# A fixed TensorE order for the first memory attention of a two-layer streaming trunk

## The chip, the cores and the metric

The kernel runs on one core of one Trainium2 chip. The metric is the device time of one execution in microseconds (us). Before the change the median of three executions is 769.24 us (768.9 to 769.38).

## The reference

Two layers over 512 tokens of width 1024. The first layer mixes tokens with a chunkwise matrix memory (mLSTM, four heads of 256), the second with block-causal attention over a compressed key/value side. Each layer also attends to a fixed memory of 256 rows with four heads of 128; the first of these two memory attentions is what the change touches:

```python
def memory_attention(mq, mz, mk, mv, q_gain):
    bsz, s, _ = mq.shape
    q = rmsnorm(mq.reshape(bsz, s, MEM_HEADS, MEM_HEAD_DIM), q_gain)
    sc = jnp.einsum("bqhd,bkhd->bhqk", q, mk, preferred_element_type=jnp.float32) * (MEM_HEAD_DIM ** -0.5)
    p = jax.nn.softmax(sc, axis=-1).astype(mv.dtype)
    out = jnp.einsum("bhqk,bkhd->bqhd", p, mv).reshape(bsz, s, MEM_WIDTH)
    return out * jax.nn.silu(mz)
```

Beside it the layer projects its normed input to q and k (convolved, with SiLU), to v, and to two gates o and z, head by head, and needs the input and forget gates of the recurrence.

## The kernel before

Precision comes from splitting: every operand of a projection is held as a high part and a low part (`split`, lines 128 to 137: ScalarE copies the high part at L130, VectorE subtracts it at L131), and a product is three matmuls, two with the high weights (L157) and one with the low ones (L162). Weights come in pieces of 512 KB (`load`), each split in the same way into two buffers that take turns (wr, wh, wl).

The work of the layer is written as Python generators that yield at places where other work may stand in between, and `weave(main, side, plan)` runs a main generator and lets a side one advance `plan[i]` steps after the main one's step `i`, one step where the plan is over. In the stretch of the change the main chain is `a_qk(0)` (four projections of 24 matmuls each, two pieces of 12 with a yield after each and one more at the end; then a convolution of four taps on VectorE, L627 and L629, and a SiLU, L200 and L201), `a_v(0)` (the value projection, four weight pieces over four token tiles) and `a_oz(0)` (the gates of head 0). The side generator is `memory_and_gates`: six steps of `mem_attn`, and in the fourth the end of the recurrence's gates (L604 to L610).

Step `i` of `mem_attn` does three things for three heads: the transposes of head `i-1`'s probabilities (`trans`, eight at L368, then two splits), the scores of head `i` (`scores`, two att tiles of 12 matmuls in all, a row maximum at L328, a bias at L330, an exponential with row sum at L338 on ScalarE, a reciprocal at L339 and a scaling at L341), and the values of head `i-2` (`values`, six matmuls and a gating at L346). The att tiles are in two PSUM buffers, the transposes' tp tiles in two others.

The generators only set the order in which the program is written down. Before the change, a scheduler then places each engine's instructions by a timeline of its own, TensorE's among them, so that matmuls of the side generator stand in the middle of projections. On the chip each engine has one queue in the order that the scheduler gave it.

Of the kernel before, what the change touches and what calls it, by code (L numbers as in the profile page):

```python
# [40 lines left out]
def weave(main, side, plan=()):  # L41
    for i, _ in enumerate(main):
        for _ in range(plan[i] if i < len(plan) else 1):
            next(side, None)
    for _ in side:
        pass


def chain(*gens):
    for g in gens:  # L50
        yield from g


def drain(g):
    for _ in g:
        pass
# [3 lines left out]
def trunk(ctx: ExitStack, tc: tile.TileContext, pv_d, pos_d, x_d, mem_d, memT_d, wmem_d, wg_d, wa_d, woa_d,  # L60
# [20 lines left out]
    def st(shape, tag, bufs=1, dt=F32):  # L81
        return POOLS.get(tag, sp).tile(shape, dt, tag=tag, bufs=bufs, name=nm(tag))

    def wide(tag, bufs, dt=F32):

        t = st([P, 1056], tag, bufs, dt)
        return t[:, :NT * 258].rearrange("p (t c) -> p t c", t=NT)
# [4 lines left out]
    def s2(shape=(P, 512)):  # L92
        return st(list(shape), "s2", NS2)

    def acc(shape=(P, 512)):
        return pp.tile(list(shape), F32, tag="acc", bufs=4, name=nm("acc"))
# [26 lines left out]
    def col(name, i=0):  # L123
        o = _PV[name] + i
        return pv[:, o:o + 1]


    def split(hi, lo, src, scale=None):
        if scale is None:
            A.activation(hi, src, AF.Copy)  # L130
            V.tensor_tensor(out=lo, in0=src, in1=hi.bitcast(F32), op=ALU.subtract)  # L131
        else:
            A.activation(hi, src, AF.Identity, scale=scale)  # L133
            V.scalar_tensor_tensor(out=lo, in0=src, scalar=scale, in1=hi.bitcast(F32),  # L134
                                   op0=ALU.mult, op1=ALU.subtract)

    def load(src, nk, ncol, pieces=1, raw=None):
        n = nk * ncol
        if raw is None:
            raw = wp.tile([P, 1024], F32, tag="wr", bufs=2, name=nm("wr"))  # L140
            nc.sync.dma_start(raw[:, :n], src)
        hi = wp.tile([P, 1024], F32R, tag="wh", bufs=2, name=nm("wh"))
        lo = wp.tile([P, 1024], F32R, tag="wl", bufs=2, name=nm("wl"))
        for i in range(pieces):
            ps_ = slice(i * n // pieces, (i + 1) * n // pieces)
            split(hi[:, ps_], lo[:, ps_], raw[:, ps_])
        return (hi[:, :n].rearrange("p (k c) -> p k c", k=nk), lo[:, :n].rearrange("p (k c) -> p k c", k=nk))
# [41 lines left out]
    def proj_T(w, hT, ps):  # L189
        for k in range(0, KT, 4):  # L190
            prod([(ps, sub(hT, slice(None), j), sub(w, slice(None), j), False) for j in range(k, k + 4)],
                 k == 0, k == 4)
            yield
# [4 lines left out]
    def silu2(out, src, t=None):  # L198
        t = s2() if t is None else t
        A.activation(t, src, AF.Tanh, scale=0.5)  # L200
        V.scalar_tensor_tensor(out=out, in0=t, scalar=1.0, in1=src, op0=ALU.add, op1=ALU.mult)  # L201
# [147 lines left out]
    def mem_attn(mu, mkT, mv, yT):  # L349
        mq, sz, rq = mu  # L350
        prs, pTs = {}, {}

        def scores(h):
            prs[h] = []
            for j in range(2):
                ps = att([P, 2, 256])
                for t in range(2):
                    tt = 2 * j + t
                    prod([(ps[:, t], sub(mq[h // 2], slice(None), h % 2, slice(tt * P, (tt + 1) * P)),
                           sub(mkT, slice(None), h), True)], True, True)  # L360
                prs[h] += softmax_rows([ps[:, 0], ps[:, 1]], rq[:, 2 * j:2 * j + 2, h])

        def trans(h):
            pT = st([P, 2, S], "s4", 2, F32R), st([P, 2, S], ("gt", "z4")[h % 2], 1, F32R)
            for kt in range(2):
                tp = tps()
                for t in range(NT):
                    PE.transpose(tp[:, t * P:(t + 1) * P], prs[h][t][:, kt * P:(kt + 1) * P], ident)  # L368
                split(pT[0][:, kt], pT[1][:, kt], tp)
            pTs[h] = pT  # L370

        def values(h):
            ps = att()
            prod([(ps, sub(pTs[h], slice(None), kt), sub(mv, slice(None), kt, slice(h * P, (h + 1) * P)), False)
                  for kt in range(2)], True, True)
            gate_out(yT, 8 + h, ps, sz[h // 2][:, h % 2])

        for i in range(6):
            if 0 <= i - 1 < 4:
                trans(i - 1)  # L380
            if i < 4:
                scores(i)
            if 0 <= i - 2 < 4:
                values(i - 2)
            yield
# [228 lines left out]
    def a_qk(h):  # L614
        i0 = 4 + 20 * (h // 2) + 12 * (h % 2)
        r = 4 + 2 * (h % 2)
        for n, name in enumerate("qk"):
            heads[h][name] = st([P, 2, S], "qk", 4, F32R), yT[n][:, r:r + 2]
        for i in range(4):
            w = load(wa_d[i0 + i], KT, P)  # L620
            ps = acc()
            yield from proj_T(w, hT, ps)
            j = (8 if i >= 2 else 0) + 2 * h + i % 2
            tmp = st([P, 2, S], "kl")
            raw, u = tmp[:, 0], tmp[:, 1]
            A.activation(raw, ps, AF.Copy)
            V.tensor_scalar(u, raw, col("cw", 48 + j), col("cb", j), op0=ALU.mult, op1=ALU.add)  # L627
            for d in range(1, 4):
                V.scalar_tensor_tensor(out=u[:, d:], in0=raw[:, :S - d], scalar=col("cw", (3 - d) * 16 + j),  # L629
                                       in1=u[:, d:], op0=ALU.mult, op1=ALU.add)  # L630
            silu2(u, u, raw)
            hi, lo = heads[h]["qk"[i // 2]]
            split(hi[:, i % 2], lo[:, i % 2], u)
            yield

    def tok_proj(i0, evac):
        pss = [acc() for _ in range(NT)]
        for c in range(4):
            w = load(wa_d[i0 + c], 2, 512)
            yield from prod_tok(pss, lambda k, t: rows(hT, k, t), w, 2, 2 * c, c == 0, c == 3, evac)  # L640

    def a_v(pr):
        vs = []
        for j in range(2):
            v = wide("v", 2, F32R), st([P, NT, 256], "u4", 5, F32R)
            G.memset(v[0][:, :, 256:258].bitcast(F32), 1.0)
            heads[2 * pr + j]["v"] = v
            vs.append(v)

        def evac(t, ps):  # L650
            for j in range(2):
                split(vs[j][0][:, t, 0:256], vs[j][1][:, t], ps[:, j * 256:(j + 1) * 256])

        yield from tok_proj(8 + 20 * pr, evac)

    def a_oz(h):
        gt = st([P, NT, 256], ("gt", "z4")[h % 2])
        heads[h]["g"] = gt

        def evac(t, ps):  # L660
            th = s2()
            A.activation(th, ps, AF.Tanh, scale=0.5)
            V.scalar_tensor_tensor(out=th[:, 256:], in0=th[:, 256:], scalar=1.0, in1=ps[:, 256:],
                                   op0=ALU.add, op1=ALU.mult)
            V.scalar_tensor_tensor(out=gt[:, t], in0=th[:, :256], scalar=1.0, in1=th[:, 256:],
                                   op0=ALU.add, op1=ALU.mult)

        yield from tok_proj(4 + 20 * (h // 2) + (8, 16)[h % 2], evac)
# [82 lines left out]
    def memory_and_gates():  # L751
        for i, _ in enumerate(mem_attn(mu, mkT, mv, yT)):
            if i == 3:
                drain(gc)
            yield

    weave(chain(a_qk(0), a_v(0), a_oz(0)), memory_and_gates(), (1, 0, 0) * 6)
    weave(chain(a_qk(1), a_oz(1)), a_attn(0))
    rope_tables()
    weave(chain(a_qk(2), a_v(1), a_oz(2)), a_attn(1))  # L760
# [414 lines left out]
```

## Time and profile before

| | us |
|---|---|
| median of three executions | 769.24 |
| the profiled execution | 769.35 |
| its span, first to last instruction | 767.6 |
| what lies around the span | 1.75 |
| TensorE busy with matmuls | 755.0 (98% of the span) |
| VectorE busy | 484.1 (63%) |
| ScalarE busy | 409.4 (53%) |

PE is TensorE's matmuls, DVE is VectorE, ACT is ScalarE, POOL is GpSimd. In rows of the timeline the first number is the start in us from the span's start, the second the duration in us, then engine, line, operation, tiles written and read, shape, and how many alike follow each other; in square brackets stands how long the engine was idle before, and what ended that. A matmul's duration reaches over the start of the next, so that the work per matmul is read from start to start.

### The profile page before, as it was taken

The page shows a single profiled execution, that of the slowest core. Times are in us where ns is not written, and L with a number is a line of the kernel's source. Part 1 is how long each engine was busy: PE and PEld are TensorE (multiplying, and loading weights), DVE is VectorE, ACT ScalarE, POOL GpSimd, SP SyncE. Part 2 cuts the span into 40 slices and gives each one's busy share as a digit, 9 for nine tenths or more (in the row PEclk, how much of TensorE's full clock was granted, in tenths as well). Part 3 has the DMA queues.
Part 4 walks back from the last instruction along what each step waited for, and adds up shares of the span by engine and source line. Part 5 has one row for each costly group of instructions (what it writes and reads, how often), then busy time and mean ns, then how long its engine had stood idle before and what let it go on. Part 6 is the DMA issues. An engine that isn't in the chain of part 4 may idle for free.

```text
span 767.6 us, 10826 instructions
## 1 busy us (share of the span) xinstructions
PE 755.0 (98%) x3948; PEld 647.8 (84%) x3948; DVE 484.1 (63%) x945; ACT 409.4 (53%) x958; POOL 106.8 (14%) x159
## 2 busy tenths in 40 slices
PE   8999998999999999999999999999999999999998
PEld 6798887888888888888888887899888888888886
DVE  5743599547868836766434664566758697776422
ACT  6964557345446435536333658457856666644220
POOL 0131010010110101001001131020334230500000
PEclk9999999999999999999999999999999999999999
DMA  9523120322132222224443532121221111511241
GB/s 323 207 84 109 56 84 29 109 83 90 63 99 80 83 89 104 71 94 154 154 160 137 174 129 73 53 83 59 83 87 59 56 50 40 190 56 56 66 155 55
DMA packets 25909, 76.39 MB, mean 100 GB/s; under 512 B 3072, under 2 KB 3968, under 8 KB 25856
## 3 DMA queue, kind: packets, MB, share of 16 engines
q1 hardware_dynamic: 24144, 73.44, 28.4%
q10 hardware_dynamic: 1584, 2.25, 0.8%
q8 instruction: 31, 0.51, 0.3%
q14 instruction: 22, 0.18, 0.1%
q0 software_dynamic: 128, 0.01, 0.0%
HBM read 71.49 MB, written 4.19 MB: 99 GB/s over the span
## 4 chain that ended last, share of the span: by engine, by line
PE 85%; DVE 8%; ACT 3%; issue 1%; DMA 1%; POOL 0%; SPq 0%; ACTq 0%; DVEq 0%
PE acc L157 47%; PE acc L162 23%; PE att L157 3%; PE att L1031 2%; PE att L162 2%; DMA yTh<-in_wmem_dram 1%; DVE wl L131 1%; PE tp L1018 1%; DVE tiny L328 1%; ACT junk L187 1%; DVE kl L629 1%; ACT s L338 1%; PE tp L952 1%; PE att L715 1%; PE att L716 1%
## 5 line engine op out<-in xcount | busy, mean ns | idle before, releaser
L131 DVE TENSOR_TENSOR wl<-wr,wh 128x1024 fp32r<-128x1024 f32 (+5 forms) x117 | 136.2, 1165 | 152.9 <-ACT wh L130 126.7
L130 ACT ACTIVATE wh<-wr 128x1024 fp32r<-128x1024 f32 (+5 forms) x117 | 117.5, 1008 | 134.1 <-PE acc L157 123.8
L157 PE MATMUL acc<-wh,hTl 128*128 128x512 f32 (+3 forms) x320 | 113.3, 365 | 0.0
L157 PE MATMUL acc<-wh,hTh 128*128 128x512 f32 (+3 forms) x320 | 112.4, 367 | 0.3 <-ACT hTh L133 0.3
L157 PE MATMUL acc<-hTh,wh 128*128 128x512 f32 x256 | 101.8, 398 | 0.0
L157 PE MATMUL acc<-hTl,wh 128*128 128x512 f32 x256 | 100.3, 392 | 0.0
L157 PE MATMUL acc<-wh,yTh 128*128 128x512 f32 (+1 forms) x224 | 84.7, 382 | 0.0
L157 PE MATMUL acc<-wh,yTl 128*128 128x512 f32 (+1 forms) x224 | 84.5, 379 | 0.0
L162 PE MATMUL acc<-wl,hTh 128*128 128x512 f32 (+3 forms) x320 | 82.0, 364 | 0.0
L162 PE MATMUL acc<-hTh,wl 128*128 128x512 f32 x256 | 69.8, 392 | 0.0
L157 PEld LDWEIGHTS acc<-wh,hTh 128*128 128x128 f32 x320 | 59.1, 188 | 9.4 <-ACT hTh L133 0.6
L157 PEld LDWEIGHTS acc<-wh,hTl 128*128 128x128 f32 x320 | 59.6, 188 | 8.7 <-DVE hTl L134 0.2
L162 PEld LDWEIGHTS acc<-wl,hTh 128*128 128x128 f32 x320 | 56.5, 188 | 8.6
L162 PE MATMUL acc<-wl,yTh 128*128 128x512 f32 (+1 forms) x224 | 60.1, 378 | 0.0
L162 PEld LDWEIGHTS acc<-hTh,wl 128*128 128x128 f32 x256 | 47.6, 188 | 9.9 <-DVE wl L131 0.2
L157 PEld LDWEIGHTS acc<-hTh,wh 128*128 128x128 f32 x256 | 48.1, 188 | 9.1
L157 PEld LDWEIGHTS acc<-hTl,wh 128*128 128x128 f32 x256 | 48.2, 188 | 9.1
L157 PEld LDWEIGHTS acc<-wh,yTh 128*128 128x128 f32 x224 | 42.1, 188 | 7.2
L157 PEld LDWEIGHTS acc<-wh,yTl 128*128 128x128 f32 x224 | 42.1, 188 | 7.1
L162 PEld LDWEIGHTS acc<-wl,yTh 128*128 128x128 f32 x224 | 41.2, 188 | 7.4
L182 POOL TENSOR_SCALAR tiny<-tiny 128x8 f32<-128x8 f32 (+3 forms) x21 | 5.5, 262 | 245.1 <-ACT junk L187 68.2
L157 PE MATMUL acc<-wh,u 128*128 128x384 f32 (+1 forms) x160 | 37.8, 362 | 0.8 <-ACT u L133 0.7
(285 smaller groups left out, 1387.0 us busy)
## 6 DMA issues: line engine op xcount, KB each, us to landing
wr<-in_wa_dram SPq DMA_DIRECT2D x46, 512.0 KB, 3.2
wr<-in_wb_dram SPq DMA_DIRECT2D x16, 512.0 KB, 3.5
wr<-in_woa_dram SPq DMA_DIRECT2D x12, 512.0 KB, 3.2
wr<-in_wob_dram SPq DMA_DIRECT2D x12, 512.0 KB, 3.2
wr<-in_wmem_dram SPq DMA_DIRECT2D x8, 512.0 KB, 3.4
yTh<-in_wmem_dram SPq DMA_DIRECT2D x5, 512.0 KB, 7.3
yTl<-in_x_dram SPq DMA_DIRECT2D x4, 512.0 KB, 9.1
u<-in_x_dram SPq DMA_DIRECT2D x4, 512.0 KB, 6.2
```

What stands on the lines that cost most here:

```text
L130: A.activation(hi, src, AF.Copy)
L131: V.tensor_tensor(out=lo, in0=src, in1=hi.bitcast(F32), op=ALU.subtract)
L157: PE.matmul(ps, x if lhs else w_[0], w_[0] if lhs else x, start=start and id(ps) not in seen, stop=False)
L162: PE.matmul(ps, a_[0] if lhs else w_[1], w_[1] if lhs else a_[0], start=False, stop=stop and left[id(ps)] == 0)
L187: A.activation(j[:, :src.shape[-1]], src, AF.Square, scale=scale, accum_out=accum)
L328: V.tensor_reduce(mx[:, j:j + 1], ps, axis=AX.X, op=ALU.max)
L338: A.activation(out[j], ps, AF.Exp, bias=nb[:, j:j + 1], scale=rq[:, j:j + 1], accum_out=sm[:, j:j + 1])
L629: V.scalar_tensor_tensor(out=u[:, d:], in0=raw[:, :S - d], scalar=col("cw", (3 - d) * 16 + j), in1=u[:, d:], op0=ALU.mult, op1=ALU.add)
L715: PE.matmul(ps[:, :258], low(c, i), v[0][:, c], start=False, stop=False)
L716: PE.matmul(ps[:, :256], ph[:, blk(c, i)], v[1][:, c], start=False, stop=c == i)
L952: PE.transpose(tp[:, t * P:(t + 1) * P], main[:, t, h * P:(h + 1) * P], ident)
L1031: PE.matmul(ps[:, i * P:(i + 1) * P], vt[:, c, h * P:(h + 1) * P], pTs[h][:, o:o + P], start=c == 0, stop=c == i)
```

## The change

The weave of the stretch is put under a manual schedule for TensorE: its instructions stay in the order in which the generators write them, and the scheduler places only the other engines around them. The plan changes too: the six steps of the memory attention come after the main chain's steps 1, 5, 9, 13, 16 and 19 (before: 1, 4, 7, 10, 13 and 16), and none after that. Steps 1 to 12 are those of `a_qk(0)`, so that step four of the memory attention now comes after the first yield of the value projection, and steps five and six later in it.

```diff
-    weave(chain(a_qk(0), a_v(0), a_oz(0)), memory_and_gates(), (1, 0, 0) * 6)
+    with tc.manual_schedule(engines={mybir.EngineType.PE}):
+        weave(chain(a_qk(0), a_v(0), a_oz(0)), memory_and_gates(), (1, 0, 0, 0) * 3 + (1, 0, 0) * 2 + (1,) + (0,) * 20)
```

The number of instructions on each engine is the same. The orders of GpSimd and of the DMA queue on SyncE are the same row for row, those of VectorE and ScalarE are the same up to head 0's softmax (VectorE's up to L600 behind the scaling of its first half), and from the gate projection of head 0 on all orders are the same again. Three places show what moved.

TensorE behind the second of the four projections (its last four matmuls are the row acc_1060 before and acc_1062 now). Before, the third projection, acc_1155, came next, and head 0's transposes, L368, only in the fourth, acc_1261:

```order
L162 MATMUL acc_1060<-hTh_171,wl_1057 128x512 x4
L157 MATMUL acc_1155<-hTh_171,wh_1151 128x512
...
L157 MATMUL att_1089<-mkT_167,u_86_471 128x256
...
L162 MATMUL acc_1155<-hTh_171,wl_1152 128x512 x4
L157 MATMUL acc_1261<-hTh_171,wh_1257 128x512
L157 MATMUL acc_1261<-hTl_172,wh_1257 128x512
L368 MATMUL tp_1075<-ident,s_178_1006 128x128
L368 MATMUL tp_1082<-ident,s_178_1006 128x128
```

The same place now, with the transposes of both halves (s_178 and s_183) and head 1's scores (att_1103, att_1122) ahead of the third projection, acc_1157:

```order
L162 MATMUL acc_1062<-hTh_171,wl_1059 128x512 x4
L368 MATMUL tp_1089<-ident,s_178_1008 128x128 x2
L368 MATMUL tp_1089<-ident,s_183_1027 128x128 x2
L368 MATMUL tp_1096<-ident,s_178_1008 128x128 x2
L368 MATMUL tp_1096<-ident,s_183_1027 128x128 x2
L157 MATMUL att_1103<-mkT_167,u_86_471 128x256
...
L157 MATMUL att_1122<-mkT_167,u_86_471 128x256
...
L157 MATMUL acc_1157<-hTh_171,wh_1153 128x512
```

Head 0's transposes moved ahead by 38 matmuls of projections, to a place where nothing else stands between them and the second projection.

TensorE behind the third projection, now: head 1's transposes (s_197, s_202), head 2's scores (att_1208, att_1227) and head 0's values (att_1246) follow each other, and only then the fourth projection, acc_1263:

```order
L162 MATMUL acc_1157<-hTh_171,wl_1154 128x512 x4
L368 MATMUL tp_1194<-ident,s_197_1115 128x128 x2
L368 MATMUL tp_1194<-ident,s_202_1134 128x128 x2
L368 MATMUL tp_1201<-ident,s_197_1115 128x128 x2
L368 MATMUL tp_1201<-ident,s_202_1134 128x128 x2
L157 MATMUL att_1208<-mkT_167,u_88_473 128x256
...
L157 MATMUL att_1227<-mkT_167,u_88_473 128x256
...
L157 MATMUL att_1246<-s_190_1087,mv_169 128x512
...
L157 MATMUL acc_1263<-hTh_171,wh_1259 128x512
```

Before, head 0's values (att_1222) came after two weight pieces of the value projection for its first two token tiles; now they stand straight behind two tiles of scores. The two att buffers are held by those scores, so att_1246 takes the buffer of att_1208. The next step repeats the pattern with att_1342, att_1361 and att_1380.

VectorE now, from the scaling of head 1's second half to the bias of head 2's first scores:

```order
L341 TENSOR_SCALAR s_202_1134<-s_202_1134,tiny_1135 128x256 x2
L201 SCALAR_TENSOR_TENSOR kl_1141<-kl_1141 128x512
L131 TENSOR_TENSOR wl_1311<-wr_1308,wh_1310 128x1024
L131 TENSOR_TENSOR z_211_1193<-tp_1194,s_210_1192 128x512
L328 TENSOR_REDUCE tiny_1215<-att_1208 128x1 x2
L131 TENSOR_TENSOR yTh_173<-kl_1141,qk_975 128x512
L131 TENSOR_TENSOR z_211_1193<-tp_1201,s_210_1192 128x512
L330 SCALAR_TENSOR_TENSOR tiny_1218<-tiny_1215,rq_477 128x2
```

Seven instructions now stand between the scaling that lets head 1's transposes go and the bias that lets the exponentials of att_1208 go.

## Rows read from the trace of the kernel before

**Rows 1.** The page: busy time and share of each engine.
```profile
PE 755.0 (98%) x3948; PEld 647.8 (84%) x3948; DVE 484.1 (63%) x945; ACT 409.4 (53%) x958; POOL 106.8 (14%) x159
```

**Rows 2.** Whom TensorE waited for, 76 to 150 us: total, times, longest.
```profile
PE att L157 <- ACT s L338: 1.5, 2, 0.8
```

**Rows 3.** Busy time by windows: us, PE, PEld, DVE, ACT, POOL, PEclk, DMA share, GB/s.
```profile
96.00:110.00 14.00, 14.00 (x76) 11.95 (x75) 13.84 (x35) 8.12 (x19) 2.29 (x4) 1.00 0.34 112
```

**Rows 4.** Timeline of PE, 92 to 152 us: the third projection's first matmuls.
```profile
96.00 0.39 PE L157 MATMUL acc<-hTh,wh 128*128 128x512 f32 x1
96.23 0.39 PE L157 MATMUL acc<-hTl,wh 128*128 128x512 f32 x1
```

**Rows 5.** Timeline of DVE, 80 to 150 us: head 0's softmax.
```profile
103.00 0.60 DVE L341 TENSOR_SCALAR s<-s,tiny 128x256 f32<-128x256 f32 x2
103.52 0.41 DVE L600 TENSOR_SCALAR e<-e 4x512 f32<-4x512 f32 x1
103.86 0.74 DVE L328 TENSOR_REDUCE tiny<-att 128x1 f32<-128x256 f32 x2
104.52 0.14 DVE L339 RECIPROCAL tiny<-tiny 128x2 f32<-128x2 f32 x1
```

**Rows 6.** Timeline of PE: the three waits, and transposes and scores without one.
```profile
121.88 1.03 PE L368 MATMUL tp<-ident,s 128*128 128x128 f32 x8
122.67 0.36 PE L157 MATMUL att<-mkT,u 128*128 128x256 f32 x1
122.87 0.28 PE L157 MATMUL att<-mkT,qk 128*128 128x256 f32 x1
122.99 0.28 PE L162 MATMUL att<-v,u 128*128 128x256 f32 x1
...
124.31 0.50 PE L157 MATMUL att<-s,mv 128*128 128x512 f32 x1 [0.69 <-ACT s L338]
124.65 0.39 PE L157 MATMUL att<-z,mv 128*128 128x512 f32 x1
...
126.38 0.63 PE L604 MATMUL tp<-ident,e 128*128 128x128 f32 x4 [0.41 <-DVE gt L131]
...
128.18 0.50 PE L157 MATMUL att<-s,mv 128*128 128x512 f32 x1 [0.83 <-ACT s L338]
...
129.66 1.03 PE L368 MATMUL tp<-ident,s 128*128 128x128 f32 x8
```

**Rows 7.** Timeline of DVE: durations of the links, and head 3's first scaling.
```profile
109.38 0.74 DVE L629 SCALAR_TENSOR_TENSOR kl<-kl,pv 128x511 f32<-128x511 f32 x1
110.04 0.15 DVE L330 SCALAR_TENSOR_TENSOR tiny<-tiny,rq 128x2 f32<-128x2 f32 x1
110.11 1.28 DVE L131 TENSOR_TENSOR gt<-tp,s 128x512 fp32r<-128x512 f32 x2
...
113.35 1.21 DVE L131 TENSOR_TENSOR wl<-wr,wh 128x1024 fp32r<-128x1024 f32 x1
...
124.69 0.61 DVE L341 TENSOR_SCALAR s<-s,tiny 128x256 f32<-128x256 f32 x2
```

**Rows 8.** Timeline of ACT, 80 to 150 us: one tile's two exponentials, and two splits.
```profile
105.82 0.55 ACT L338 ACTIVATE s<-att,tiny,rq 128x256 f32<-128x256 f32 x1
...
106.81 0.20 ACT L338 ACTIVATION_READ_ACCUMULATOR s<-att,tiny,rq 128x1 f32 x1
...
108.11 1.08 ACT L130 ACTIVATE s<-tp 128x512 fp32r<-128x512 f32 x2
```

**Rows 9.** The last matmuls, and busy time and PEclk by windows at the end.
```profile
763.30 0.61 PE L162 MATMUL acc<-wl,yTh 128*128 128x512 f32 x2
...
766.00:766.50 0.50, 0.00 (x0) 0.00 (x0) 0.00 (x0) 0.00 (x0) 0.00 (x0) 1.00 0.42 156
...
767.00:767.60 0.60, 0.00 (x0) 0.00 (x0) 0.00 (x0) 0.00 (x0) 0.00 (x0) 0.50 0.00 0
```

**Rows 10.** Timeline of PE, 0 to 34 us: the first transposes.
```profile
1.81 4.34 PE L121 MATMUL tp<-ident 128*128 128x128 f32 x20 [1.81 <-POOL ident masks.py:199]
```

## The prediction

> **What bounds the kernel now.** I read the page's busy times first: TensorE works through 755.0 of 767.6 us [rows 1]. So the change, which moves matmuls and adds or removes none, can gain no more than TensorE's idle time, and all that it makes TensorE wait is lost, unless a later wait shrinks by it. Next the waits of the stretch in which the orders differ: two waits for ScalarE's exponentials, 1.5 us together [rows 2]; the timeline has them at 124.31 and 128.18 (0.69 and 0.83 us) with a third, 0.41 us, between them at 126.38 [rows 6]. That is the prize. Then the other engines there: from 96 to 110 us VectorE is busy for 13.84 of 14 us [rows 3], so a link of a softmax is done when its turn comes in VectorE's queue, not when its inputs are there. A fixed TensorE order is judged by that: where does TensorE now arrive before VectorE?
>
> **What goes.** The waits of 0.69, 0.41 and 0.83 us, 1.93 in all. After a wait the next matmul starts 0.34 us on (124.31 to 124.65) where 0.23 is the pace [rows 4, 6], so each costs 0.11 more: 2.3 us (an estimate). The moved matmuls cost the same elsewhere. DMAs and GpSimd keep their orders; weight pieces follow TensorE through their two buffers, so what TensorE loses they lose too, and nothing is fetched further ahead.
>
> **First new wait: head 0's transposes.** Behind the second projection TensorE stood at 96.00 before, and began the third [rows 4]. The work up to there is the same set of matmuls, so now it stands at 96.00 before the transposes. They read what L341 writes, and VectorE writes the first half at 103.00 to 103.60 [rows 5]. Nothing of VectorE's queue up to there moved, nor waits for what TensorE does after 96. Then comes L600 (to 103.86, where the next started), and as the two row maxima of 103.86 (0.66 us) now stand later, the reciprocal (0.14) and the second pair of L341 (0.60) end at about 104.65. Two of the eight transposes go at about 103.5, two by 104.75, the other four by 105.15, and with 0.1 at the change back to scores, head 1's scores start at 105.3. Without waiting they would start 0.79 + 0.09 after 96.00, at 96.9 (eight transposes take 121.88 to 122.67, and the first score's 0.20 is 0.08 over the 0.12 of the next) [rows 6]. Loss: **8.4 us**. Before, the third projection and half of the fourth filled this time; now they stand behind the transposes.
>
> That loss needs the projections to stay behind. The trace shows it: at 128.18 TensorE ended 0.83 us of waiting for one matmul, while the transposes behind it, whose first inputs VectorE had scaled by 125.3 [rows 7], started only at 129.66 [rows 6]. The Trainium skill, "TensorE: Matmul & The Clock Gate", section "Step-by-step: what each phase is for", says why one might hope otherwise: TensorE pulls weight loads ahead, but the matmuls "stay in program order". If more than loads could pass, the sum would be the 2.3 us gained; the rows side with the page's second half.
>
> **Second: head 1's transposes.** Scores (12 by 0.12) and the third projection (24 by 0.23) bring TensorE from 105.3 to 112.2. VectorE meanwhile needs, from 104.65: L201 (taken as a split beside it, 0.60), three splits of 0.60 to 0.65, three taps L629 (0.66 each), L627, two pairs of row maxima (0.66 each), and the scalings [rows 5, 7]; in the new order the second pair of L341 ends near 113.2. Loss: **0.9 us** (0 to 1.5).
>
> **Third: head 0's values, att_1246.** From that scaling, E, TensorE needs five transposes, twelve scores and 0.1: it stands before att_1246 at E + 2.0. Its buffer is free once both exponentials have read att_1208. VectorE first: L201 0.60, the weight split 1.13, a split 0.60, a pair of maxima 0.66, two splits 1.2, L330 0.1 [rows 5, 7], 4.3 in all, some 0.15 of it late; then two exponentials on ScalarE, 105.82 to 107.01, 1.2 [rows 8]. With 0.11 for resuming that is E + 5.8. Loss: **3.8 us**. Before, matmuls of the value projection stood here.
>
> **Fourth: head 1's values, att_1380.** From the start F of head 2's transposes, which by then wait for nothing, TensorE needs 0.88 + 1.42 = 2.3. The chain: four transposes and their end 0.65, ScalarE's split 0.55 [rows 8], two splits and a pair of maxima on VectorE 1.9, L201 and L330 0.7, a ScalarE split behind it 0.55, two exponentials 1.2, resuming 0.15: F + 5.7, and up to 0.5 more because the taps of the fourth projection's convolution stand ahead in VectorE's queue. Loss: **3.7 us** (3.3 to 4.0). Later steps find their inputs ready: two weight pieces of the value projection stand between the rest.
>
> Sum: 8.4 + 0.9 + 3.8 + 3.7 - 2.3 = 14.5 us.
>
> **The clock.** The trace of before has no wait of TensorE over 1.8 us [rows 10] until the end. There the granted clock, 1.00 (2.4 GHz), still stands at 766.5, and is 0.50 (1.2 GHz) from 767.0 on, with TensorE idle since 763.9 [rows 9]: it fell within 3.1 us. The first new wait has about 7.4 us without a matmul, more than twice as long as that, so I expect the clock at its lower level when TensorE resumes. For the price of a restart the one row is the kernel's first 20 transposes, 4.34 us or 0.21 each [rows 10], where later ones take 0.10 [rows 6]; 20 at that pace would take 2.0, so the slow stretch cost 2.3. Ends: 0 (it rises at once, or the slow part falls into the next wait) and 2.3; I take 2.0, since the scores and the projection after this wait depend on TensorE alone. The Trainium skill, same page, section "HAM oscillation — how this bites in real kernels", has the rule that work after a long wait starts cold; the 0.50 at the end agrees, and no row here shows it for work that follows. For the waits of 3.8 and 3.7 us I take nothing, though they are a little longer than the 3.1 of the end; that is a rival.
>
> So 14.5 + 2.0 = 16.5 us. The profiled execution took 769.35, so it would take 785.85; the median of three is 0.11 lower, and my number for it is **785.7 us**.
>
> **Rivals.**
> - *The clock falls in every long wait.* Two more restarts at 2.0: 789.7. For it: 3.7 and 3.8 exceed 3.1. Against: by little. The rule of the Trainium skill cited above, "HAM oscillation — how this bites in real kernels" in "TensorE: Matmul & The Clock Gate", read strictly, is this case. Chance 0.17.
> - *The clock costs nothing.* 783.7. For it: no row shows a slow matmul after the first 6 us. Against: the 0.50 at the end. Chance 0.13.
> - *Only the first wait stays.* VectorE and ScalarE gain on TensorE while it stands, and the others shrink to nothing: 8.4 - 2.3 gives 775.3. For it: ScalarE is idle for 47% of the span [rows 1]. Against: the third and fourth are chains that start at TensorE's own scores and transposes, so a head start doesn't shorten them. Chance 0.07.
> - *Faster: head 0 is ready in time.* If L341 came before 96, TensorE would meet scaled rows at each step, the three waits would go and none come: 769.24 - 2.3 = 766.9. It decides at head 0's first L341, which must come 7 us earlier. Against: the 38 matmuls that covered this are gone and VectorE's queue ahead of it is the same row for row. Chance 0.02.
> - *Nothing changes*, because the order is undone when the program is built: the order shown is that of the built program. Chance 0.01.
>
> **How the numbers follow.** The forecast has 0.60; with the first two rivals 0.90. Its terms give 783 to 788 (second wait 0 to 1.5, fourth 3.3 to 4.0, clock 0 to 2.3), and the rivals with most chance end at 789.7; below, the third and fourth waits could each be 1.5 us shorter where ScalarE's turn comes sooner. Range 780.5 to 790. About 0.2% (1.5 us) is what a measurement of this kernel can tell from no change. Slower 0.97, within 0.01, faster 0.02.
>
> **What would show it.** In the changed profile: a wait of TensorE at L368 for VectorE's L341 of about 7 us ending near 103.4; two waits of att L157 for ScalarE's L338 of 3 to 4 us each, near 115 to 119 and 131 to 136; the granted clock at 0.50 behind the first; no wait at L604; all after about 165 us shifted as one. Wrong if the first wait is under 4 us, if the row of head 0's L341 stands before 100, or if later waits shrink as much as these grow.

## The result and the profile after

The changed kernel takes **787.28 us** (median of four executions, 786.35 to 788.09) against 769.31 of the kernel before: a ratio of 1.0229, 95% interval 1.0216 to 1.0241. The forecast was 785.7 in a range of 780.5 to 790.0; the sign, the places and the size hold, but its terms missed in both directions, and these misses cancel in part. The profiled execution took 786.35 us with a span of 784.6, so the rows below explain 17.0 us (784.6 - 767.6). Behind the stretch everything is shifted as one: a later matmul with the same place in both orders starts at 195.19 where it started at 178.19, 17.0 later, as the end does.

The page's first row, which answers to [rows 1]: the same number of matmuls.

```profile
PE 759.9 (97%) x3948; PEld 652.1 (83%) x3948; DVE 485.5 (62%) x945; ACT 410.5 (52%) x958; POOL 107.5 (14%) x159
```

The waits of TensorE from 76 to 180 us (in all, times, longest), which answer to [rows 2]: the wait at L604 is gone, and there are three long ones, 7.3 us (and 0.3 right behind it) at the transposes, 3.0 and 3.5 at the values.

```profile
PE tp L368 <- DVE s L341: 7.6, 2, 7.3
PE att L157 <- ACT s L338: 6.5, 2, 3.5
```

TensorE's timeline, which answers to [rows 4, 6]:

```profile
94.75 1.07 PE L162 MATMUL acc<-hTh,wl 128*128 128x512 f32 x4
103.13 0.66 PE L368 MATMUL tp<-ident,s 128*128 128x128 f32 x2 [7.32 <-DVE s L341]
104.10 1.59 PE L368 MATMUL tp<-ident,s 128*128 128x128 f32 x6 [0.31 <-DVE s L341]
105.34 0.56 PE L157 MATMUL att<-mkT,u 128*128 128x256 f32 x1
105.70 0.41 PE L157 MATMUL att<-mkT,qk 128*128 128x256 f32 x1
...
108.05 0.52 PE L157 MATMUL acc<-hTh,wh 128*128 128x512 f32 x1
...
113.65 1.03 PE L368 MATMUL tp<-ident,s 128*128 128x128 f32 x8
114.44 0.36 PE L157 MATMUL att<-mkT,u 128*128 128x256 f32 x1
...
115.82 0.28 PE L162 MATMUL att<-v,u 128*128 128x256 f32 x1
119.08 0.79 PE L157 MATMUL att<-s,mv 128*128 128x512 f32 x1 [2.98 <-ACT s L338]
...
121.80 0.47 PE L157 MATMUL acc<-hTh,wh 128*128 128x512 f32 x1
...
132.25 0.28 PE L162 MATMUL att<-v,u 128*128 128x256 f32 x1
136.04 0.79 PE L157 MATMUL att<-s,mv 128*128 128x512 f32 x1 [3.52 <-ACT s L338]
...
138.77 0.73 PE L604 MATMUL tp<-ident,e 128*128 128x128 f32 x4
```

The first wait ends at 103.13, with VectorE's row of head 0's L341 (102.65 to 103.25, below); head 1's transposes at 113.65 wait for nothing; the values wait at 119.08 and 136.04. Each of the three waits is followed by matmuls at half the pace: eleven scores from 105.70 to 108.05, 0.21 each, where 0.12 is the pace of those without a wait [rows 6]. The third projection, which TensorE began at 96.00 before [rows 4], stands behind all this at 108.05.

What ended the first and the third wait, from VectorE's and ScalarE's timelines, which answer to [rows 5, 7] and [rows 8]:

```profile
102.65 0.60 DVE L341 TENSOR_SCALAR s<-s,tiny 128x256 f32<-128x256 f32 x2
103.17 0.41 DVE L600 TENSOR_SCALAR e<-e 4x512 f32<-4x512 f32 x1
...
103.69 0.61 DVE L341 TENSOR_SCALAR s<-s,tiny 128x256 f32<-128x256 f32 x2
...
105.50 0.69 DVE L131 TENSOR_TENSOR gt<-tp,s 128x512 fp32r<-128x512 f32 x1 [0.60 <-ACT s L130]
...
112.22 0.62 DVE L341 TENSOR_SCALAR s<-s,tiny 128x256 f32<-128x256 f32 x2
```

```profile
118.38 0.55 ACT L338 ACTIVATE s<-att,tiny,rq 128x256 f32<-128x256 f32 x1
118.83 0.20 ACT L338 ACTIVATION_READ_ACCUMULATOR s<-att,tiny,rq 128x1 f32 x1
```

Head 0's row is where it was before (102.65 against 103.00 [rows 5]), and TensorE now stands there before it. Head 1's second half is scaled by 112.84, and TensorE, slowed, comes for it at 113.65. The values of 119.08 go when the second exponential of the older scores tile has been read out, at 119.03.

The granted clock in windows (columns as in [rows 3]): 1.00 is the level of 2.4 GHz, 0.50 that of 1.2 GHz.

```profile
103.00:105.30 2.30, 1.86 (x8) 1.49 (x9) 1.87 (x6) 1.24 (x4) 0.00 (x0) 0.50 0.65 226
105.30:108.10 2.80, 2.80 (x15) 2.80 (x14) 2.60 (x6) 1.77 (x4) 0.00 (x0) 0.50 0.00 0
108.10:113.60 5.50, 5.50 (x25) 4.55 (x25) 5.22 (x15) 3.59 (x10) 0.00 (x0) 0.98 0.00 0
...
119.00:122.00 3.00, 2.92 (x7) 2.35 (x8) 2.96 (x9) 1.51 (x6) 0.00 (x0) 0.50 0.02 5
122.00:130.00 8.00, 8.00 (x37) 6.60 (x36) 5.07 (x9) 3.13 (x5) 0.00 (x0) 1.00 0.02 3
...
136.00:139.80 3.80, 3.76 (x15) 2.89 (x15) 2.35 (x10) 1.15 (x5) 0.00 (x0) 0.60 0.00 0
139.80:150.00 10.20, 10.20 (x50) 8.57 (x50) 3.72 (x7) 3.85 (x6) 0.00 (x0) 1.00 0.17 53
```

The clock is at its lower level when TensorE resumes after each of the three long waits, not only after the first, and comes back while it works.

### The profile page after: what moved, and what is told of

Same layout as the page of the kernel before. It is cut to its first block, busy times and chain, and to the rows that moved or that the text cites. A ratio compares the mean times of both kernels' runs of the same rounds, so it can differ in the third digit from the quotient of the medians.

```text
span 784.6 us, 10828 instructions
## 1 busy us (share of the span) xinstructions
PE 759.9 (97%) x3948; PEld 652.1 (83%) x3948; DVE 485.5 (62%) x945; ACT 410.5 (52%) x958; POOL 107.5 (14%) x159
## 4 chain that ended last, share of the span: by engine, by line
PE 84%; DVE 8%; ACT 5%; issue 1%; DMA 1%; POOL 0%; ACTq 0%; DVEq 0%; POOLq 0%
PE acc L157 47%; PE acc L162 23%; PE att L157 4%; PE att L162 2%; PE att L1032 2%; DVE wl L131 1%; ACT junk L187 1%; ACT wh L130 1%; PE tp L1019 1%; PE tp L368 1%; PE tp L953 1%; ACT s L338 1%; DVE tiny L328 1%; PE att L715 1%; PE att L716 1%
## 5 line engine op out<-in xcount | busy, mean ns | idle before, releaser
L130 ACT ACTIVATE wh<-wr 128x1024 fp32r<-128x1024 f32 (+5 forms) x117 | 117.6, 1008 | 145.2 <-PE acc L157 135.2
```

## The experiments

The theory: the order that the generators write puts links of a softmax straight behind each other on TensorE, so it waits for VectorE's and ScalarE's part of the chain, and each long wait costs a slow restart beside it. Rivals: the new shares are to blame and not the fixed order; VectorE's queue bounds the stretch, so that a wait which is taken away comes back elsewhere; the clock costs nothing. Ratios are against the kernel before on the same chip, whose median is 769.3 to 769.6 us; where a median is set against that of the changed kernel, the chips are different ones, and these 0.3 us lie between them.

**1. The shares alone, or the fixed order alone.** The first kernel has the new shares and no manual schedule:

```diff
-    with tc.manual_schedule(engines={mybir.EngineType.PE}):
-        weave(chain(a_qk(0), a_v(0), a_oz(0)), memory_and_gates(), (1, 0, 0, 0) * 3 + (1, 0, 0) * 2 + (1,) + (0,) * 20)
+    weave(chain(a_qk(0), a_v(0), a_oz(0)), memory_and_gates(), (1, 0, 0, 0) * 3 + (1, 0, 0) * 2 + (1,) + (0,) * 20)
```

> The new plan of shares without the hand-fixed order: the scheduler again places TensorE's instructions. My theory (the fixed order makes TensorE stand where the scheduler would have put projection work): 768 to 771, no wait of TensorE over 2 us from 76 to 180 us. Rival (the plan itself, by asking for the value projection late, costs part of it): 775 or more, with waits at the attention's values left.

769.52 us, ratio 0.9999 (0.9989 to 1.0009). From 76 to 180 us TensorE waits 1.5 us for ScalarE at the values and 0.4 at L604, as before [rows 2, 6].

The second has the manual schedule and the old shares:

```diff
-        weave(chain(a_qk(0), a_v(0), a_oz(0)), memory_and_gates(), (1, 0, 0, 0) * 3 + (1, 0, 0) * 2 + (1,) + (0,) * 20)
+        weave(chain(a_qk(0), a_v(0), a_oz(0)), memory_and_gates(), (1, 0, 0) * 6)
```

> The hand-fixed order with the old shares (1,0,0)*6: only the fixing, not the new shares. My theory (any order written in program order puts head 0's transposes right behind the second projection, before VectorE has scaled their rows): 784 to 791, with a first wait of 7 to 9 us at L368 for L341 and two long ones at the values. Rival (the new shares are what hurts, a fixed order alone is harmless): 768 to 772.

790.63 us, ratio 1.0271 (1.0254 to 1.0288), with the same three waits, the first and the first of those at the values longer (8.9 and 3.8 us in place of 7.3 and 3.0), the last one 3.5 us as in the changed kernel:

```profile
PE tp L368 <- DVE s L341: 9.2, 2, 8.9
PE att L157 <- ACT s L338: 7.3, 2, 3.8
```

So the whole loss comes with the fixed order. The new shares, taken with it, give 3.4 us back (790.63 - 787.28). They put head 0's transposes one weight piece later; the waits are 2.4 us shorter, and the slow stretch behind the first values is 3.0 us long where it is 6.2 with the old shares (granted clock 0.50 from 119.8 to 126.0).

**2. The values ahead of the next transposes and scores.**

```diff
         for i in range(6):
+            if 0 <= i - 2 < 4:
+                values(i - 2)
             if 0 <= i - 1 < 4:
                 trans(i - 1)
             if i < 4:
                 scores(i)
-            if 0 <= i - 2 < 4:
-                values(i - 2)
             yield
```

> In each step of the memory attention the values of the head before the last now come ahead of the next transposes and scores. My theory (waits three and four are a chain: scores, ScalarE's exponentials, buffer of att free): those two waits of 3.0 and 3.5 us go, with their slow clock, and the first of 7.3 us stays: 776 to 780, that is 8 to 11 us under the changed kernel. Rival (VectorE's queue bounds this stretch, so what is not waited for there is waited for at the next place): 784 to 788, the waits come back at L368 or L604.

779.77 us, 7.5 under the changed kernel. Both waits at the values are gone; head 0's values go straight behind the third projection:

```profile
103.55 0.66 PE L368 MATMUL tp<-ident,s 128*128 128x128 f32 x2 [7.31 <-DVE s L341]
...
105.76 0.56 PE L157 MATMUL att<-mkT,u 128*128 128x256 f32 x1
...
108.47 0.63 PE L157 MATMUL acc<-hTh,wh 128*128 128x512 f32 x1
...
114.62 0.39 PE L157 MATMUL att<-s,mv 128*128 128x512 f32 x1
```

What was taken away is worth 3.1 + 1.45 + 3.7 + 1.5 = 9.75 us by the rows of after; 7.5 were gained. Of the rest 1.1 is a new wait at L609, which now comes right behind L604, and some 0.55 lies in the first restart, which costs 2.5 us here (below) and 1.95 in the changed kernel. That leaves 8.1. The rows have 8.0: from the end of the second projection to the same later matmul it is 95.66 to 195.19 in the changed kernel and 96.09 to 187.62 here. So the chain of scores, exponentials and att buffers is the cause of these two waits, and the rival's return is small here.

**3. The clock.** TensorE is kept at work in the long waits with transposes of the identity into a tile that nobody reads:

```diff
+        def busy(n):
+            if n:
+                ps = tps()
+                for _ in range(n):
+                    PE.transpose(ps[:, 0:P], ident, ident)
...
         def trans(h):
+            busy(fill.get(("T", h)))
...
         def values(h):
+            busy(fill.get(("V", h)))
...
-        for i, _ in enumerate(mem_attn(mu, mkT, mv, yT)):
+        for i, _ in enumerate(mem_attn(mu, mkT, mv, yT, {("T", 0): 70, ("V", 0): 26, ("V", 1): 32})):
```

> 128 transposes of the identity, whose results nobody reads, are added in TensorE's three long waits (70, 26 and 32 of them), so that TensorE keeps working while the same work is late. They add no output. Theory that each fall of the clock costs 1.1 to 1.4 us here: the granted clock stays 1.00 from 86 to 150 us, and the time is 2 to 4 us under the changed kernel, 783 to 785.5. Rival (VectorE's queue sets the end of the stretch whatever TensorE's clock is): the clock stays 1.00 and the time is within 1 us of the changed kernel, 786.3 to 788.3.

783.43 us, 3.85 under the changed kernel, with 128 more matmuls. The granted clock over the whole stretch, and TensorE's timeline (L367 is the added work, L375 the transposes that are L368 elsewhere):

```profile
86.00:150.00 64.00, 62.87 (x379) 54.33 (x378) 49.63 (x111) 32.88 (x67) 2.40 (x5) 1.00 0.16 52
```

```profile
95.17 7.80 PE L367 MATMUL tp<-ident 128*128 128x128 f32 x70
102.80 0.38 PE L375 MATMUL tp<-ident,s 128*128 128x128 f32 x2
103.60 1.03 PE L375 MATMUL tp<-ident,s 128*128 128x128 f32 x6 [0.41 <-DVE s L341]
104.39 0.36 PE L157 MATMUL att<-mkT,u 128*128 128x256 f32 x1
...
105.88 0.39 PE L157 MATMUL acc<-hTh,wh 128*128 128x512 f32 x1
...
111.38 0.50 PE L375 MATMUL tp<-ident,s 128*128 128x128 f32 x2
112.19 1.03 PE L375 MATMUL tp<-ident,s 128*128 128x128 f32 x6 [0.31 <-DVE s L341]
112.97 0.36 PE L157 MATMUL att<-mkT,u 128*128 128x256 f32 x1
...
114.35 0.28 PE L162 MATMUL att<-v,u 128*128 128x256 f32 x1
...
118.09 0.50 PE L157 MATMUL att<-s,mv 128*128 128x512 f32 x1
...
129.92 0.28 PE L162 MATMUL att<-v,u 128*128 128x256 f32 x1
...
133.72 0.50 PE L157 MATMUL att<-s,mv 128*128 128x512 f32 x1
```

The added work does not set the ends of the waits: at the first, TensorE stands idle for VectorE once more behind it (0.41 us at 103.60), and at the third ScalarE has read the scores tile out at 118.04, just before the values start. This is the sum of the prediction without a clock. Its four waits are 104.39 - 95.17 - 0.88 = 8.3, then 112.97 - 111.38 - 0.79 = 0.8, then 118.09 - 114.47 = 3.6 and 133.72 - 130.04 = 3.7 us (0.12 after the start of the last score). With the 2.3 removed that is 14.1, where the prediction had 14.5 and the medians differ by 14.0 (783.43 - 769.46). From the end of the second projection to the same later matmul (95.17 to 191.53) it takes 96.4 us, 3.2 less than the changed kernel; the medians have 3.85. The second wait is back as soon as the clock holds.

The same for the one long wait that the order of experiment 2 has left (its filler of 70, and values first):

> The order with the values first (the two waits at the values gone) and 70 transposes of the identity, whose results nobody reads, in the one long wait that is left. Theory that one fall of the clock costs 2.2 to 2.5 us of TensorE's own work (transposes 0.6, scores 1.2, projection 0.7, as the run with the values first shows it): granted clock 1.00 from 86 to 150 us, 1.5 to 3 us under the run with the values first, 776.8 to 778.3. Rival (VectorE takes it back): within 1 us of that run, 778.8 to 780.8.

777.86 us, 1.9 under experiment 2, with the clock at 1.00 from 86 to 150 us. One restart there cost 2.5 us by rows of experiments 2 and 3: 0.6 in the transposes (103.55 to 105.76, against 102.80 to 104.39), 1.2 in the scores (2.71 against 1.49) and 0.65 in the projection (6.15 against 5.50, 108.47 to 114.62 and 105.88 to 111.38). Some of it came back: TensorE now waits 0.4 us for L346 that it did not meet before.

**4. Does each wait stand for itself?** The first part of the gates, small work of VectorE (and, as the trace shows, of ScalarE) ahead of head 0's softmax, is issued later:

```diff
-    next(gc)
...
         for i, _ in enumerate(mem_attn(mu, mkT, mv, yT)):
+            if i == 1:
+                next(gc)
```

> The changed kernel with one move: the first part of the gates (small scans and sums on VectorE, 7 us of its queue) is issued inside the memory attention's second step and no longer ahead of it, so head 0's rows are scaled earlier. Theory that each wait stands for itself: the first wait of 7.3 us goes with its slow clock, the others stay: 776 to 780. Theory that VectorE's queue as a whole sets when the heads are done (the work moved stands ahead of a later link): the first wait goes, the waits at the values grow by about as much, the time stays within 3 us of the changed kernel, 784 to 790.

785.10 us, 2.2 under the changed kernel. The waits:

```profile
PE att L157 <- ACT s L338: 12.4, 2, 8.9
PE tp L368 <- DVE s L341: 0.6, 1, 0.6
```

```profile
106.66 0.68 DVE L574 SCALAR_TENSOR_TENSOR e<-s 4x512 f32<-4x512 f32 x1 [1.26 <-ACT s L571]
```

The wait of 7.3 us at L368 is nearly gone, and that at head 0's values has grown from 3.0 to 8.9: the work that was moved stands ahead of the row bias of head 2's scores in VectorE's queue. So the place of a wait is TensorE's order's doing, but shortening one link here lengthens a later one. The move is not VectorE's alone: the gates bring ScalarE's logarithm (L571) into the stretch, with two table loads of 1.28 us (at 104.61 and 107.73; in the changed kernel both come before 93), and VectorE waits 1.26 and 0.41 us for ScalarE there. How much of the 8.9 us is VectorE's queue and how much ScalarE's, this run does not separate.

The other way to shorten the first wait is to place head 0's transposes later on TensorE, behind the third projection:

```diff
-        weave(chain(a_qk(0), a_v(0), a_oz(0)), memory_and_gates(), (1, 0, 0, 0) * 3 + (1, 0, 0) * 2 + (1,) + (0,) * 20)
+        weave(chain(a_qk(0), a_v(0), a_oz(0)), memory_and_gates(), (1, 0, 0, 0, 0, 0, 0, 0, 1, 0, 0, 1, 0, 1, 0, 0, 1, 0, 0, 1) + (0,) * 20)
```

> Still TensorE's order fixed by hand; only the shares move the second step (head 0's transposes and head 1's scores) behind the third projection, and the steps after it to main steps 12, 14, 17 and 20. Theory that each wait stands for itself: the first shrinks by the projection's 5.5 us to about 2 and the clock does not fall there, some 7 us off the changed kernel: 779 to 781. Theory that VectorE's and ScalarE's queues set when the heads are done: 2 to 4 us off, 783 to 785.5, the rest coming back as waits at the values and at the value projection's acc buffers for ScalarE.

783.62 us, 3.7 under the changed kernel. The waits, and the clock in windows:

```profile
PE att L157 <- ACT s L338: 8.1, 2, 4.1
PE tp L368 <- DVE s L341: 2.3, 2, 1.9
```

```profile
104.00:105.20 1.20, 1.00 (x8) 0.87 (x9) 1.20 (x3) 1.20 (x3) 0.00 (x0) 1.00 0.69 277
105.20:108.50 3.30, 3.30 (x16) 3.11 (x15) 3.30 (x7) 1.35 (x3) 0.00 (x0) 0.53 0.43 159
...
119.90:125.80 5.90, 5.83 (x14) 4.63 (x15) 5.08 (x13) 3.00 (x8) 0.00 (x0) 0.50 0.00 0
```

TensorE idles 5.3 us less at L368, and 1.6 more at the values; the slow stretch behind the third wait is 5.9 us long where it was 3.0, and the clock falls behind the transposes too, which the first theory excluded. The time is the one that the theory of the queues gave, but the waits at the value projection's acc buffers that it named did not come.

**5. Better than both?** Two kernels take work off VectorE in the order of the kernel before. One takes the two row maxima of a scores tile in one instruction, the other scales the rows on GpSimd:

```diff
-    def softmax_rows(rows_, rq):
+    def softmax_rows(rows_, rq, both=None):
...
-        for j, ps in enumerate(rows_):
-            V.tensor_reduce(mx[:, j:j + 1], ps, axis=AX.X, op=ALU.max)
+        V.tensor_reduce(mx, both, axis=AX.X, op=ALU.max)
...
-                prs[h] += softmax_rows([ps[:, 0], ps[:, 1]], rq[:, 2 * j:2 * j + 2, h])
+                prs[h] += softmax_rows([ps[:, 0], ps[:, 1]], rq[:, 2 * j:2 * j + 2, h], ps)
```

```diff
-    def softmax_rows(rows_, rq):
+    def softmax_rows(rows_, rq, fin=None):
...
-            V.tensor_scalar(out[j], out[j], sm[:, j:j + 1], None, op0=ALU.mult)
+            (fin or V).tensor_scalar(out[j], out[j], sm[:, j:j + 1], None, op0=ALU.mult)
...
-                prs[h] += softmax_rows([ps[:, 0], ps[:, 1]], rq[:, 2 * j:2 * j + 2, h])
+                prs[h] += softmax_rows([ps[:, 0], ps[:, 1]], rq[:, 2 * j:2 * j + 2, h], G)
```

> The kernel before (scheduler's order) with the two row maxima of a pair of the memory attention taken by one VectorE instruction over 128x2x256 in place of two of 128x256. By the 0.41 us of one and the 0.54 to 0.74 of rows with 512 elements it saves 0.1 us for each of 8 pairs in a stretch that VectorE fills from 96 to 134 us. Theory that VectorE bounds this stretch also before: 0.2 to 0.8 us faster than before. Rival (TensorE's order alone bounds it): within 0.2 us of before, or up to 0.5 slower since both exponentials of a pair now start behind one maximum.

> The kernel before with the scaling of the memory attention's softmax rows (L341, 16 of 0.34 us on VectorE) on GpSimd, which is idle there. By GpSimd's 0.72 us for 128x128 at L269 one 128x256 takes 1 to 1.4 us there. Theory that VectorE's load bounds this stretch: 0.2 to 1.5 us faster than before. Rival (each head's chain gets 1.5 us longer and TensorE waits for it): same to 2 us slower, with waits at L368 for GpSimd.

769.18 us, ratio 0.9995 (0.9986 to 1.0004), and 771.14, ratio 1.0018 (1.0009 to 1.0027). One maximum for both takes 0.68 us where two take 0.74 [rows 5], TensorE still waits 1.4 us in the stretch (1.9 before), and no difference can be measured. On GpSimd a scaling takes 1.32 us in place of 0.34. The waits at L368 for GpSimd that the rival named did not come: TensorE waits 1.84 us once, at the values for L338, no more than before in three waits. The profiled execution, 769.77, is the fastest of its eleven, so the trace does not show where the median loses 1.6 us. GpSimd's group from 96 to 140 us:

```profile
L341 POOL TENSOR_SCALAR s<-s,tiny 128x256 f32<-128x256 f32 x16 | 20.9, 1321 | 8.0 <-DVE tiny L339 8.0
```

No version here beats the kernel before. Whether a fixed order with the links cut finer could was not tried.

## Why the prediction was right, and where it was not

| term, us | predicted | after | how it is read |
|---|---|---|---|
| waits removed | -2.3 | -2.3 | none is left |
| first wait | 8.4 | 8.2 | 95.66 + 0.88 to 105.34 is 8.8, less 0.6 in slow transposes |
| its clock | 2.0 | 1.95 | that 0.6; scores 2.71, at the full clock 1.50; projection 5.60 for 5.47 |
| second wait | 0.9 | 0 | TensorE comes at 113.65, the rows are scaled by 112.84 |
| third wait | 3.8 | 3.1 | 115.94 to 119.08 |
| its clock | 0 | 1.45 | values 2.72 us, 1.38 at the pace of 0.23, and 0.1 behind them |
| fourth wait | 3.7 | 3.7 | 132.37 to 136.04 |
| its clock | 0 | 1.5 | values 2.73 us, 1.38 at that pace, and 0.14 at L604 and L609 |
| sum | 16.5 | 17.6 | |

TensorE came to the first wait at 95.66 (94.75 and four matmuls) and not at 96.00, 0.3 in its favour: 17.3, against 17.0 in the spans. The median lies 1.0 higher against before's; the profiled execution is the fastest of the four. That the sums differ by only 1.1 is in part luck: 2.95 us too little for the clock, 1.85 too much for the waits and the first restart.

- **Right: the first wait.** It is at L368, for L341, ends at 103.1, and nothing passes it. The step "TensorE stands before VectorE's row of 103.0" was the whole argument, and the row moved by only 0.35 us.
- **Right in size: the price of that restart**, taken from the kernel's first 20 transposes [rows 10]: 2.0 against 1.95. Their pace, 0.21 each, is that of the six at 0.50 here (104.10 to 105.34), though the granted clock reads 1.00 over them. So close a match is luck: the price goes by what stands behind the wait, 2.5 where nothing there can wait (experiment 3), 1.45 and 1.5 behind the other two.
- **Right: the fourth wait**, and at the full clock the third (3.6). Both are made by the order of values and scores (experiment 2).
- **Wrong: "For the waits of 3.8 and 3.7 us I take nothing."** The clock fell in both, at 2.95 us together. The rival for this, at a chance of 0.17, had the condition right but priced each at 2.0: here only the six matmuls of the values and little behind them run at the lower level. Behind the wait of 4.0 us with the transposes later (experiment 4), seven matmuls of the value projection are slow as well (122.69 to 125.68).
- **Wrong: the second wait.** It was worked out with TensorE at full pace between the first and it. The slow scores use up its time, and experiment 3 shows it back at 0.8. The clock's terms and this one overlap: gross the clock costs 4.9 us (1.95 + 1.45 + 1.5), net 3.85 by the medians with the clock kept up, 3.2 by the rows. The forecast of 0.9 is itself not covered by its terms: the links of VectorE named for it come to some 7.3 to 7.8 us, not to the 8.55 from 104.65 to 113.2. The queue did take 8.54 us (104.30 to 112.84), since VectorE waited 0.60 in it for ScalarE's L130, which the sum does not name; that 0.8 came with the clock held is so far luck.
- **Wrong in size: the third wait**, 3.1 for 3.8. It is a race between TensorE and a chain that began with VectorE's last scaling; TensorE came 1.1 us later to it than reckoned (0.8 of it at head 1's transposes, which it met all scaled), and the chain was some 0.4 us longer, as VectorE waited 0.60 us in it for ScalarE's copy of a weight piece (L130). With the clock held the chain takes 5.7 us from VectorE's scaling (112.40 to 118.09), the 5.8 of the prediction.
- **Half right: "only the first wait stays."** The argument against that rival, that a head start does not shorten a chain which begins at TensorE's own scores, holds; its price, 775.3, leaves out the restart of 2.0 behind the same wait. What experiment 4 adds is that the queues of VectorE and ScalarE tie the waits together: of the first wait and its clock, some 10 us, moving the gates gave back 2.2, and placing the transposes later 3.7.

On the clock the Trainium skill, "TensorE: Matmul & The Clock Gate", section "HAM oscillation — how this bites in real kernels", has the rule that work after each long wait starts cold, and it counts the extra time as half of the slow stretch. All three waits here agree with the first half of it. For the wait that ends at 119.08, with 0.50 from 119.0 to 122.0, an estimate by that rule is 1.5 us, and 1.45 is what the rows give; for the first wait the half of 103.0 to 108.1 is 2.6, against 1.95, and TensorE was idle for 0.44 us of that stretch, which explains a part of the difference.

## What to carry to other kernels

Before an order is fixed by hand, set down for each link of a chain when its engine's queue gets to it, and put other work of the waiting engine in between; a scheduler that places matmuls of one stage inside another was worth all of the 18 us here. A wait has a second price, the slow restart, which falls on whatever stands next and may hide the next wait: sum the waits in order, with the clock in the sum, not each for itself. If the queues of other engines tie several waits together, mending one moves a part of it to the next: 1.6 of 5.3 us and 5.9 of 7.0 us here.

## What was not expected of the hardware

The clock also fell behind shorter idle times than that at the end of the kernel before (3.1 us [rows 9]). With the transposes later (experiment 4), TensorE was idle for 1.87 and 0.47 us, and had been at work again for a microsecond at 1.00 when the clock fell: 1.00 from 104.0 to 105.2, 0.53 from 105.2 to 108.5. A single wait of 1.84 us for L338, in the kernel with the scaling on GpSimd, brought no fall (1.00 in every window from 76 to 150 us). And filling a wait with work that does nothing made the kernel 3.85 us faster than leaving TensorE idle.
